# Layer norm statistics from the output tiles instead of beside the convolution taps

## The chip, the cores and the metric

The kernel runs on one core of a Trainium2 chip. What counts is the time of one execution on the device, in microseconds.

## What is computed

One layer of an encoder on two batches, 512 and 1024 tokens, with 16 meta tokens in front of each. All is in float32; matrix products are done as three products of a high and a low part.

```
u = rms_norm(h, pre_g)
z = u @ w_in                     # c_val, c_glu, c_gate, q, k, v, a_gate, 1024 columns each
y = depthwise_conv31(c_val * sigmoid(c_glu)) + conv_b
conv = silu(layer_norm(y, ln_g, ln_b)) * silu(c_gate)    # layer norm over the 1024 channels
att = neighbourhood_attention(q, k, v, rel_bias) * silu(a_gate)
out = h + rms_norm([conv ; att] @ w_out, post_g)
```

## The kernel before

In the projections and the convolution, channels lie on partitions (8 chunks `c` of 128) and the 1536 tokens lie along the free dimension, in three segments of 512. The layer norm needs a mean and a variance over channels, so over partitions and over the 8 chunks.

Stage 1, prenorm (to 100 us): the tokens are normalised, transposed and split.

Stage 2, convolution (100 to 650 us): for each chunk `c`, `stream` lets TensorE project (value, gate, the `v` of attention, the gates), while `convolve` runs the 31 taps of the chunk whose gated values `ub` are ready, each tap one pass of VectorE over 128 x 1536. The first tap (L268) and the three border copies of 15 columns (L250, L261, L262) are on ScalarE. The mean over the channels of chunk 0 is taken once by a matmul with `ones` (`conv_mean`, into `m0`); `conv_stats` subtracts it from each chunk's result (zc, which goes to DRAM as `zs`), squares that on ScalarE and adds zc and its square into `acc` and `accsq`, on GpSimd for chunks 0 to 6 and on VectorE for chunk 7. After the first projection of attention six matmuls with a column of `ones` (L538) sum both over partitions into DRAM (`std`).

Stage 3, attention (690 to 1180 us): eight pairs of heads; TensorE also projects q and k of the next pair and the gates. Results go to DRAM (`mad`). The last two gates, `a_gate(6, 7)`, are six units of 24 matmuls behind the last product with values.

Stage 4, output (from 1217 us): 12 tiles of 128 tokens. `mix` loads the sums of a tile (`moments`), the convolution half (`zs`, `cgd`) and the attention half (`mad`, `agd`) into one buffer each (`mx`, `gt`, one pair for each half), normalises, applies the gates and splits into `mh` and `ml`, which are double buffered by `t % 2`. `product` multiplies with the 16 weight blocks, whose splits (`load_wo`) are made while the last gates run. Tiles 0 and 1 are multiplied together, half by half. From tile 2 on `ml` is made on GpSimd (`MLT = 2`).

The program is traced in the order of the code; a scheduler then fixes each engine's queue by its own estimate of times. `tc.issue_after(x)` keeps the instructions of a block that are on x's engine behind x. Engines take their queues in order. All DMAs are on SP's queue.

## Time and profile before

| what | value |
|---|---|
| runs, median (lowest to highest of 3) | 1490.44 us (1488.64 to 1491.67) |
| profiled execution, its own time | 1491.02 us |
| its span, first to last instruction | 1489.2 us |
| TensorE, VectorE, ScalarE, GpSimd busy | 1444.3, 1014.3, 598.6, 321.5 us |
| mean granted TensorE clock | 0.987 of full speed |

The durations come from the profiled execution, and sums are made against its own time. A busy TensorE means that a matmul was under way; matmuls are pipelined, so the distance from start to start tells more than the duration of one.

### The profile page before, as it was taken

What the parts mean: (1) busy time and instruction counts of PE and PEld (TensorE: products, weight loads), DVE (VectorE), ACT (ScalarE), POOL (GpSimd) and SP (SyncE); (2) the same over time, 40 slices, a digit from 0 to 9 for tenths busy, and PEclk for the clock granted to TensorE, in tenths of its full rate; (3) what the DMA queues carried; (4) which work ended last, traced back from release to release, by engine and by line L of the source; (5) the groups of instructions that cost most, each with busy time, mean ns of one, the idle gap of its engine ahead of it and who ended that gap; (6) DMA issues with size and microseconds to landing.
All of it is one profiled execution on the core that took longest, in us unless ns stands there. A gap on an engine that the chain in (4) does not pass through costs nothing.

```text
span 1489.2 us, 24000 instructions
## 1 busy us (share of the span) xinstructions
PE 1444.3 (97%) x9506; PEld 1242.1 (83%) x9506; DVE 1014.3 (68%) x1713; ACT 598.6 (40%) x1323; POOL 321.5 (22%) x230
## 2 busy tenths in 40 slices
PE   7999999999989999979999999999999999999998
PEld 6988998888988887857889888888888778888886
DVE  6599989898989898974655656556555465534341
ACT  7321122111211112114545555455454576666650
POOL 2042353304220423203111110111111001221220
PEclk9999999999999999989999999999999999999999
DMA  8112213121312221213212222222122483655441
GB/s 265 38 49 92 68 49 114 40 91 47 116 46 84 68 91 57 92 50 94 64 57 73 64 63 72 75 64 73 48 78 86 154 293 114 187 144 167 121 142 43
DMA packets 124469, 138.90 MB, mean 93 GB/s; under 512 B 8110, under 2 KB 96430, under 8 KB 124356
## 3 DMA queue, kind: packets, MB, share of 16 engines
q1 hardware_dynamic: 124356, 137.36, 30.1%
q8 instruction: 74, 1.21, 0.3%
q14 instruction: 39, 0.32, 0.1%
HBM read 99.05 MB, written 42.71 MB: 95 GB/s over the span
## 4 chain that ended last, share of the span: by engine, by line
PE 61%; DVE 6%; DMA 1%; ACT 1%; POOL 1%; issue 1%; DVEq 0%; SPq 0%; ACTq 0%
PE mm L179 25%; PE py L796 18%; PE ss L615 5%; DVE z L270 4%; PE po L653 4%; PE tp L637 4%; PE tp L179 3%; PE po L179 2%; DMA wraw<-in_wo 1%; PE mm L333 1%; POOL acc L293 0%; DMA yo<-in_wo 0%; DVE accsq L294 0%; POOL accsq L294 0%; DVE uw L745 0%
## 5 line engine op out<-in xcount | busy, mean ns | idle before, releaser
L179 PE MATMUL mm<-uw,whi 128*128 128x512 f32 (+2 forms) x1904 | 559.6, 373 | 11.0 <-DVE kl L506 11.0
L270 DVE SCALAR_TENSOR_TENSOR z<-ub,cw_sb,z 128x1536 f32<-128x1536 f32 (+2 forms) x270 | 511.4, 1901 | 39.9 <-ACT z L268 31.9
L179 PEld LDWEIGHTS mm<-uw,whi 128*128 128x128 f32 x1904 | 344.2, 190 | 70.0 <-issue 13.6
L179 PE MATMUL mm<-uw,wlo 128*128 128x512 f32 (+2 forms) x952 | 354.5, 372 | 4.0 <-POOL wlo L141 4.0
L141 POOL TENSOR_TENSOR wlo<-wraw,whi 128x1024 fp32r<-128x1024 f32 x48 | 126.9, 2645 | 450.4 <-ACT whi L140 440.3
L179 PEld LDWEIGHTS mm<-uw,wlo 128*128 128x128 f32 x952 | 180.5, 190 | 32.2 <-POOL wlo L141 4.8
L796 PE MATMUL py<-uw,mh 128*128 128x512 f32 x576 | 178.4, 391 | 0.0
L179 PE MATMUL tp<-uw,whi 128*128 128x512 f32 (+2 forms) x512 | 133.9, 345 | 0.0
L626 ACT ACTIVATE pt<-pt,sm 128x216 f32<-128x216 f32 (+4 forms) x192 | 97.4, 508 | 78.4 <-DVE sm L625 76.6
L796 PEld LDWEIGHTS py<-uw,mh 128*128 128x128 f32 x576 | 108.1, 188 | 23.6
L796 PE MATMUL py<-uw,ml 128*128 128x512 f32 x288 | 112.5, 391 | 0.0
L622 DVE CUSTOM_DVE_ANT_0 pt<-ss,ei 128x216 f32<-128x216 f32 (+2 forms) x144 | 62.7, 438 | 64.8 <-PE ss L615 45.1
L639 ACT COPY pT<-tp 108x256 f32<-108x256 f32 (+4 forms) x192 | 79.3, 424 | 64.6 <-PE tp L637 55.5
L179 PEld LDWEIGHTS tp<-uw,whi 128*128 128x128 f32 x512 | 89.4, 188 | 12.1 <-issue 0.5
L776 POOL TENSOR_TENSOR ml<-mx,mh 128x1024 fp32r<-128x1024 f32 x20 | 49.2, 2480 | 218.4 <-ACT mh L775 218.4
L333 PE MATMUL mm<-vh,uw 128*128 128x256 f32 x448 | 87.6, 291 | 7.3 <-ACT vs L336 4.8
L769 DVE TENSOR_TENSOR mx<-mx,mb 128x1024 f32<-128x1024 f32 x12 | 16.8, 1399 | 104.8 <-DMA mx<-zs 104.8
L179 PE MATMUL tp<-uw,wlo 128*128 128x512 f32 (+2 forms) x256 | 88.1, 344 | 0.0
L637 PE MATMUL tp<-ident,pt 128*96 128x128 f32 (+2 forms) x480 | 87.5, 276 | 0.3
L628 DVE TENSOR_SCALAR pt<-pt,sm 128x216 f32<-128x216 f32 (+4 forms) x192 | 81.6, 427 | 5.4
L333 PEld LDWEIGHTS mm<-vh,uw 128*128 128x128 f32 x448 | 72.9, 197 | 9.3 <-ACT vs L336 5.4
L627 DVE RECIPROCAL sm<-sm 128x1 f32<-128x1 f32 x192 | 31.2, 163 | 70.1 <-ACT pt L626 67.3
(184 smaller groups left out, 2265.1 us busy)
## 6 DMA issues: line engine op xcount, KB each, us to landing
wraw<-in_w_main SPq DMA_DIRECT2D x48, 512.0 KB
xt<-in_xn SPq DMA_DIRECT2D x12, 512.0 KB
vd<-vs SPq DMA_DIRECT2D x96, 64.0 KB
cgd<-ag SPq DMA_DIRECT2D x24, 256.0 KB
zs<-zc SPq DMA_DIRECT2D x24, 256.0 KB
agd<-ag SPq DMA_DIRECT2D x24, 256.0 KB
mad<-mo SPq DMA_DIRECT2D x24, 256.0 KB
mx<-zs SPq DMA_DIRECT2D x12, 512.0 KB
```

What stands on the lines that cost most here:

```text
L141: eng.tensor_tensor(out=lo, in0=raw, in1=hi.bitcast(F32), op=ALU.subtract)
L179: last_mm[0] = nc.tensor.matmul(ps[:, :n], lhsT=w[:, dc, :], rhs=u[dc // 4][:, dc % 4, :], start=(dc == 0 and i == 0), stop=(dc == DC - 1 ...
L270: nc.vector.scalar_tensor_tensor(out=zv, in0=ub[:, a:b, k:k + 512], scalar=cw_sb[:, c, k:k + 1], in1=zv, op0=ALU.mult, op1=ALU.add)
L333: nc.tensor.matmul(ps[:, :256], lhsT=u[dc // 4][:, dc % 4, :], rhs=w[dc // 4][:, dc % 4, :], start=(dc == 0 and i == 0), stop=(dc == DC - ...
L615: last_qk[0] = nc.tensor.matmul(ss[:, :nk * w], lhsT=q[:, jj].rearrange("p h x -> p (h x)"), rhs=k[:, b0:b0 + nk, ra:ra + rn, :].rearrange ...
L622: nc.vector.tensor_tensor_reduce(out=pv.rearrange("p (k x) -> p k x", k=nk), in0=sv_, in1=e.rearrange("p k r c -> p k (r c)"), scale=1.0, ...
L626: last[0] = nc.scalar.activation(out=pv, in_=pv, func=AF.Exp, bias=sm[:, 1:2], scale=1.0, accum_out=sm[:, 2:3])
L628: nc.vector.tensor_scalar(out=pv, in0=pv, scalar1=sm[:, 3:4], scalar2=None, op0=ALU.mult)
L637: nc.tensor.transpose(out=tp[:kt, k * 128:k * 128 + 128], in_=pv[:, k * kt:k * kt + kt], identity=ident)
L639: nc.scalar.copy(out=pT[:kt, :nt * 128], in_=tp[:kt, :nt * 128])
L653: last_pv[0] = nc.tensor.matmul(po[hs, j, :], lhsT=v, rhs=pT[:kt, k * 128 + h * 64:k * 128 + h * 64 + 64], start=(k == 0), stop=(k == nt - ...
L796: nc.tensor.matmul(pss[hf], lhsT=m[e // 8][:, e % 8], rhs=w[e][:, hf * 512:hf * 512 + 512], start=(n == 0 and i == 0), stop=(n == 15 and i ...
```

## The change

The sums beside the taps go: `conv_mean`, `conv_stats`, `acc`, `accsq`, `m0`, `std` and the six matmuls. A chunk's result is only reordered by a copy on ScalarE and stored (`store_z`). In the output stage each tile's convolution half is loaded, summed over its 8 chunks by a VectorE reduction, and over partitions by a 128-column matmul with `ones` (now 1/1024), which leaves the mean on every partition; it is subtracted, the result squared on ScalarE, reduced and summed by a second matmul, and the tile is normalised (`moment_1`, `moment_2`, `normalize`). These steps for tile t+1 are put between the products of tile t, at weight blocks 2 and 10. For tiles 0 and 1 they stand between the six units of the last gates. The first tap and the border copies go to VectorE, and `ml` of the convolution half is made on VectorE in all tiles.

```diff
-                    nc.scalar.copy(out=ub[:, 1, 0:15], in_=ub[:, 0, 0:15])
+                    nc.vector.tensor_copy(out=ub[:, 1, 0:15], in_=ub[:, 0, 0:15])
...
-        nc.scalar.activation(out=zv, in_=ub[:, a:b, 0:512], func=AF.Identity, scale=cw_sb[:, c, 0:1], bias=cb_sb[:, c:c + 1])
+        nc.vector.tensor_scalar(out=zv, in0=ub[:, a:b, 0:512], scalar1=cw_sb[:, c, 0:1], scalar2=cb_sb[:, c:c + 1],
+                                op0=ALU.mult, op1=ALU.add)
...
-    def conv_mean(z):
...
-    def conv_stats(c, z, i, eng):
...
+    def store_z(c, z, i):
         zc = zpool.tile([128, 512], F32, name="zc", bufs=3)
+        nc.scalar.copy(out=zc.rearrange("p (b r c) -> p b r c", r=8, c=8), in_=z[:, i].rearrange("p (r b c) -> p b r c", r=8, b=8))
         nc.sync.dma_start(zs[i][c], zc)
...
+        if c > 0:
+            for _ in conv_taps(c, z, 0, 3):
+                yield TAP_US
+        for i in range(3):
+            store_z(c, z, i)
...
-    for i in range(3):
-        sl = slice(i * 512, i * 512 + 512)
-        for k, src in enumerate((acc, accsq)):
...
-    def moments(t):
...
-    def mix(t, parts=(0, 1)):
...
+    def channel_mean():
+
+        ps = stat[0].tile([128, 512], F32, name=stat[1], tag=stat[1])
+        nc.tensor.matmul(ps[:, :128], lhsT=ones, rhs=ms[:, 0], start=True, stop=True)
+        return ps[:, :128]
+
+    def moment_1():
+        nc.vector.tensor_reduce(out=ms[:, 0], in_=mxs[0].rearrange("p c t -> p t c"), op=ALU.add, axis=mybir.AxisListType.X)
+
+    def moment_2(t):
+        mx = mxs[0]
+        sq = wpool.tile([128, DC, 128], F32, name="wraw", tag="wraw", bufs=2)
+        mean = channel_mean()
+        nc.vector.tensor_tensor(out=mx, in0=mx, in1=mean.unsqueeze(1).broadcast_to([128, 8, 128]), op=ALU.subtract)
+        nc.scalar.activation(out=sq, in_=mx, func=AF.Square)
+        nc.vector.tensor_reduce(out=ms[:, 0], in_=sq.rearrange("p c t -> p t c"), op=ALU.add, axis=mybir.AxisListType.X)
+
+    def normalize():
+        mx, rstd = mxs[0], ms[:, 1]
+        var = channel_mean()
+        nc.scalar.activation(out=rstd, in_=var, func=AF.Sqrt, bias=eps_sb[:, 1:2])
         nc.vector.reciprocal(rstd, rstd)
...
+        (nc.gpsimd if part and t >= MLT else nc.vector).tensor_tensor(out=ml, in0=mx, in1=mh.bitcast(F32), op=ALU.subtract)
...
+    def last_gate():
+        with tc.issue_after(last_pv[0] if last_tail[0] is None else last_tail[0]):
+            next(tail, None)
+        last_tail[0] = last_mm[0]
...
+    with tc.issue_after(last[0].ins):
+        load_mix(0, 0)
+        moment_1()
+    last_gate()
+    with tc.issue_after(last_tail[0]):
+        moment_2(0)
+    last_gate()
+    with tc.issue_after(last_tail[0]):
+        normalize()
+    finish_mix(0, 0)
+    for n in range(2):
         load_wo(n)
+    last_gate()
+    load_mix(1, 0)
+    moment_1()
+    for n in range(2, 6):
+        load_wo(n)
+    last_gate()
+    with tc.issue_after(last_tail[0]):
+        moment_2(1)
+    mix_attention(0)
+    last_gate()
+    with tc.issue_after(last_tail[0]):
+        normalize()
+    last_gate()
+    finish_mix(1, 0)
...
+    def moments(t, n, first, second):
+
+        if t < TG // 128 and n in (first, second):
+            with tc.issue_after(last_y[0]):
+                if n == first:
+                    moment_2(t)
+                else:
+                    normalize()
...
+                if (part, t) == (1, 0):
+                    moments(2, n, 10, 15)
...
-            mix(t)
+            finish_mix(t, 0)
+            mix_attention(t)
+            begin_mix(t + 1)
...
             for n in range(16):
+                moments(t + 1, n, 2, 10)
                 product(t, pss, n, 0)
```

## Rows read from the trace of the kernel before

**Rows 1.** Windows by stage: TensorE, its loads, VectorE, ScalarE, GpSimd busy us (instructions); clock, DMA, GB/s.
```profile
100.00:650.00 550.00, 538.81 (x3089) 471.38 (x3088) 511.34 (x290) 101.14 (x181) 167.39 (x81) 0.99 0.23 73
650.00:690.00 40.00, 29.58 (x124) 20.91 (x125) 15.00 (x33) 14.38 (x31) 9.85 (x26) 0.83 0.28 86
...
1150.00:1217.60 67.60, 63.04 (x430) 51.75 (x429) 32.75 (x59) 37.60 (x62) 3.53 (x2) 0.95 0.63 210
1217.60:1482.60 265.00, 264.95 (x1152) 217.35 (x1152) 114.60 (x158) 153.61 (x243) 49.21 (x20) 0.99 0.46 138
```

**Rows 2.** Timeline of TensorE: start us, us, instruction, [idle before it <-what ended that].
```profile
295.45 0.38 PE L333 MATMUL mm<-vh,uw 128*128 128x256 f32 x1 [1.91 <-ACT vs L336]
...
587.20 0.80 PE L179 MATMUL mm<-uw,wlo 128*128 128x512 f32 x1 [3.50 <-POOL wlo L141]
...
660.42 0.76 PE L179 MATMUL mm<-uw,whi 128*128 128x512 f32 x1 [11.04 <-DVE kl L506]
```

**Rows 3.** Windows behind two of the four waits, columns as in rows 1 (443.6 and 587.0 repeat the first).
```profile
296.80:300.20 3.40, 3.40 (x17) 3.30 (x17) 3.33 (x3) 0.38 (x1) 0.00 (x0) 0.50 0.70 221
...
660.40:665.50 5.10, 5.08 (x12) 4.03 (x13) 0.90 (x2) 0.18 (x1) 0.00 (x0) 0.50 0.00 0
```

**Rows 4.** Timeline of VectorE and of ScalarE around the last convolution chunk.
```profile
581.15 0.68 DVE L255 TENSOR_TENSOR ub<-tp,sg 128x512 f32<-128x512 f32 x1
585.98 64.44 DVE L270 SCALAR_TENSOR_TENSOR z<-ub,cw_sb,z 128x1536 f32<-128x1536 f32 x30 [4.16 <-ACT z L268]
...
583.66 0.63 ACT L292 ACTIVATE zq<-zc 128x512 f32<-128x512 f32 x1 [3.13 <-POOL accsq L294]
...
651.24 0.63 ACT L292 ACTIVATE zq<-zc 128x512 f32<-128x512 f32 x1 [17.92 <-DVE zc L287]
```

**Rows 5.** Chain that ended last, in order of time: start us, us, what; two taps.
```profile
596.18 3.85 DVE z L270
600.05 1.83 DVE z L270
```

**Rows 6.** Timeline of TensorE: the first of the statistics matmuls and what follows the fourth.
```profile
673.99 1.02 PE L538 MATMUL ss<-acc,ones 128*1 128x512 f32 x2
...
677.51 0.50 PE L179 MATMUL mm<-uw,whi 128*128 128x512 f32 x1
```

**Rows 7.** Groups by line in one tile of the output stage: busy us, mean ns; idle before.
```profile
L796 PEld LDWEIGHTS py<-uw,mh 128*128 128x128 f32 x48 | 9.0, 188 | 1.9
...
L772 ACT ACTIVATE mx<-mx,lb_sb,lg_sb 128x128 f32<-128x128 f32 x8 | 3.2, 483 | 0.1
...
L773 ACT ACTIVATE gt<-gt 128x1024 f32<-128x1024 f32 x2 | 2.1, 1060 | 2.0 <-DMA gt<-cgd 2.0
...
L757 DVE RECIPROCAL mb<-mb 128x128 f32<-128x128 f32 x2 | 1.9, 946 | 0.5 <-ACT mb L756 0.5
...
L769 DVE TENSOR_TENSOR mx<-mx,mb 128x1024 f32<-128x1024 f32 x1 | 1.2, 1225 | 10.7 <-DMA mx<-zs 10.7
```

**Rows 8.** Timeline of SP's DMA queue and of VectorE in the output stage.
```profile
1315.48 0.36 SPq L766 DMA_DIRECT2D mx<-zs  x1
...
1319.28 1.23 DVE L769 TENSOR_TENSOR mx<-mx,mb 128x1024 f32<-128x1024 f32 x1 [12.48 <-DMA mx<-zs]
...
1233.67 0.36 SPq L766 DMA_DIRECT2D mx<-zs  x1
...
1238.83 1.23 DVE L769 TENSOR_TENSOR mx<-mx,mb 128x1024 f32<-128x1024 f32 x1 [4.33 <-DMA mx<-zs]
...
1253.62 3.31 DVE L769 TENSOR_TENSOR mx<-mx,mb 128x1024 f32<-128x1024 f32 x1 [6.38 <-DMA mx<-zs]
```

**Rows 9.** Timeline of ScalarE: a table load and the activation behind it.
```profile
1217.62 1.28 ACT L756 ACT_TABLE_LOAD   x1
1218.91 0.41 ACT L756 ACTIVATE mb<-mb,eps_sb 128x128 f32<-128x128 f32 x1
```

**Rows 10.** Groups by line, 1180 to 1218 us: a weight block's cast.
```profile
L744 ACT CAST uw<-wraw 128x1024 fp32r<-128x1024 f32 x6 | 6.3, 1052 | 5.4 <-DMA wraw<-in_wo 5.4
```

More of the change, by code (lines that the diff above doesn't have):

```diff
@@ L401, in tile_encoder @@
         pass
-    m0 = zpool.tile([128, TG], F32, name="m0")
-    acc = zpool.tile([128, TG], F32, name="acc")
-    accsq = zpool.tile([128, TG], F32, name="accsq")
-    nc.gpsimd.memset(acc, 0.0)
-    nc.gpsimd.memset(accsq, 0.0)
     def stream(c):
@@ L530, in tile_encoder @@
     pair_q(0, 0)
-    for i in range(3):
-        sl = slice(i * 512, i * 512 + 512)
-        for k, src in enumerate((acc, accsq)):
-            pool, tag = ((ps_s, "ss"), (ps_t, "tp"))[k]
-            ps = pool.tile([128, 512], F32, name=tag, tag=tag)
-            nc.tensor.matmul(ps[0:1], lhsT=ones[:, 0:1], rhs=src[:, sl], start=True, stop=True)
-            row = gpool.tile([128, 512], F32, name="ag", tag="ag", bufs=2)
-            nc.scalar.copy(out=row[0:1], in_=ps[0:1])
-            nc.sync.dma_start(std[k:k + 1, sl], row[0:1])
     es1.close()
@@ L700, in tile_encoder @@
             between(p, g * 2 + hf)
-    with tc.issue_after(last_pv[0]):
-        for _ in a_gate(6, 7):
-            pass
     es2.close()
-    es_ps.close()
-    ps_y = ctx.enter_context(tc.tile_pool(name="ps_y", bufs=6, space=bass.MemoryType.PSUM, reuse_waits="tile"))
     wop = ctx.enter_context(tc.tile_pool(name="wop", bufs=1, reuse_waits="tile"))
@@ L778, in tile_encoder, with load_mix @@
[L778 to L788 removed]
+    stat = [ps_s, "ss"]
+    def load_mix(t, part):
+        g, csl = t // 4, slice(t % 4 * 128, t % 4 * 128 + 128)
+        nc.sync.dma_start(mxs[part], (zs, mad)[part][g][:, :, csl].rearrange("c p t -> p c t"))
+        nc.sync.dma_start(gts[part], (cgd, agd)[part][g][:, :, csl].rearrange("c p t -> p c t"))
@@ new lines, in normalize, with finish_mix @@
+    def normalize():
+        mx, rstd = mxs[0], ms[:, 1]
+        var = channel_mean()
+        nc.scalar.activation(out=rstd, in_=var, func=AF.Sqrt, bias=eps_sb[:, 1:2])
+        nc.vector.reciprocal(rstd, rstd)
+        nc.vector.tensor_tensor(out=mx, in0=mx, in1=ms[:, 1:2].broadcast_to([128, 8, 128]), op=ALU.mult)
+        for c in range(8):
+            nc.scalar.activation(out=mx[:, c], in_=mx[:, c], func=AF.Silu, scale=lg_sb[:, c:c + 1], bias=lb_sb[:, c:c + 1])
+    def finish_mix(t, part):
+        mx, gt = mxs[part], gts[part]
+        mh, ml = [x[t % 2 * 2 + part] for x in (mhs, mls)]
+        nc.scalar.activation(out=gt, in_=gt, func=AF.Silu)
+        nc.vector.tensor_tensor(out=mx, in0=mx, in1=gt, op=ALU.mult)
+        nc.scalar.copy(out=mh, in_=mx)
+        (nc.gpsimd if part and t >= MLT else nc.vector).tensor_tensor(out=ml, in0=mx, in1=mh.bitcast(F32), op=ALU.subtract)
@@ new lines, in tile_encoder @@
+    finish_mix(0, 0)
+    for n in range(2):
+        load_wo(n)
+    last_gate()
[12 more added lines that the diff above has]
+    finish_mix(1, 0)
+    for n in range(6, 10):
+        load_wo(n)
+    mix_attention(1)
+    for n in range(10, 16):
+        load_wo(n)
```

89 lines of the change are left out of this document (20 added, 69 removed).

## Prediction

> **What bounds the kernel now.** I read the windows by stage first, then the rows around each place where TensorE stands, and last one tile of the output stage. The windows show that TensorE is nearly always busy, and where it is not: the convolution stage (100 to 650 us) leaves it 11.2 us idle, the 40 us behind it 10.4 us, the passage into the output stage 4.6 us, and the output stage nothing, 264.95 of 265.0 us [rows 1]. So time can be won only where TensorE waits, runs at half clock, or does work that goes away, and every microsecond put in front of it later is lost again.
>
> The waits stand at the ends of convolution chunks. At 587.20 a weight load waits 3.50 us for GpSimd's weight split, at 295.45 a value projection waits 1.91 us for a PSUM copy on ScalarE (the same, 1.90 us, stands at 443.25), and at 660.42 the K projection waits 11.04 us for VectorE [rows 2]. Behind each such wait the granted clock reads 0.50, the lower level of 1.2 GHz, for 3.4 us, and for 5.1 us behind the last [rows 3]. Why they wait is seen in the chunk's end: GpSimd adds zc and its square into accumulators, ScalarE's second Square waits 3.13 us for that, and the first tap stands behind the Square on ScalarE; VectorE waits 4.16 us for it. The 30 taps then take 64.44 us, and behind them come the subtraction and, on VectorE, the last accumulations; ScalarE stood 17.92 us behind the Square that needs them, with the K evictions queued after it [rows 4].
>
> **The change, part by part.** It removes first taps (8) and Squares (24) from ScalarE, 24 subtractions and 6 accumulations from VectorE, 42 accumulations from GpSimd, and 18 matmul records from TensorE. It adds 8 first taps and 24 border copies to VectorE, 24 reordering copies to ScalarE, and in the output stage, for each of 12 tiles, two reductions, a subtraction and a Square, and two matmuls of 128 columns with `ones`.
>
> *End of chunks, gain.* With GpSimd's accumulators gone, nothing on ScalarE stands between the last gated piece and the first tap. The three earlier waits make 1.91 + 1.90 + 3.50 = 7.3 us, and half of 3 x 3.4 us at half clock is 5.1 us: 12.4 us. For chunk 7: VectorE's last gated piece ends at 581.8 [rows 4], and 30 taps at the undisturbed pitch of 1.86 us would be 55.7 us; the 8.7 us beyond that come with the weight splits on GpSimd (a tap of 3.85 us instead of 1.83 while one ran [rows 5]), of which four remain, some 8 us. The first tap on VectorE has no row; the two-input tap of 1536 elements took 1.83 us, which bounds it from above; with the border copies I take 1.5. So the taps end near 581.8 + 1.5 + 55.7 + 8 = 647, instead of 650.4, and 9 us of subtraction and accumulation no longer follow. TensorE, 5 us earlier itself, comes to this point at about 644 instead of 649. What is late next is ScalarE: the three copies that store z wait for the last tap in its queue, with the K evictions behind them, about 2 us. I therefore leave 3 us of the 11.04 and drop the half clock behind it (half of 5.1): 10.6 us. Bounds for this block: 10 us (only the early waits go) to 26 us (everything goes). Taken: 23.0 us.
>
> *Matmuls removed.* Four records with `accsq` and `acc` follow each other from 673.99 to 677.51, 0.44 us a record, 12 of them [rows 6]; the six of the mean have the same 512 columns: 18 x 0.44 = 7.9 us, all on TensorE's queue while it is otherwise full.
>
> *Work added under cover.* Border copies and first taps (8 x 1.5 = 12 us) go to VectorE, which stands idle for 39 of 550 us of the convolution stage [rows 1] and loses the subtractions. The cover is the taps finishing before TensorE needs the K evictions; without it each us there is a us.
>
> *Matmuls added.* 24 times two records of 128 columns. By columns, a quarter of 2 x 0.44 is 0.22 us; with both weight loads of 0.19 us [rows 7] in the open, 0.60. TensorE loads ahead, but a load is longer than the 0.11 us of such a record, so I take 0.40: 9.6 us (5.3 to 14.4).
>
> *Tile loop of the output stage.* This decides the sign. The statistics of tile t+1 are inserted in TensorE's queue while it multiplies tile t, and all of it goes through one buffer mx. The chain from one first statistics matmul to the next: to the second one 8 steps of three products at 265.0 / 1152 = 0.23 us plus one statistics matmul, 5.9 us (the subtraction 1.23, a Square like the Silu of 1.06, and a reduction priced like a two-input pass, 1.22, fit in that). Then the matmul's result 0.45 (an estimate from its 0.40), Sqrt 0.41 [rows 9], reciprocal 0.95, product 1.22, eight Silus 3.2, gate product 1.22 [rows 7], cast 1.05 [rows 10], ml 1.22: 9.7 us; then the load of the next mx, and a reduction, 1.2 again; with the handovers 17.1 us and the load. The load took 3.80 us from issue (1315.48) to use, and 5.16 from 1233.67 beside another load [rows 8]. Sum: 20.9 to 22.3 us. TensorE's tile takes 22.1 + 0.8 = 22.9. So the loop fits, but with 0.6 to 2.0 us to spare, and the queues hold other work: the attention half, the output's squares, gains and sums, and the ml of the attention half on GpSimd, beside which a 1.23 us pass of VectorE took 3.31 [rows 8]. I take 0.6 us of stall on each of 9 tiles, 5 us (0 to 30).
>
> A table load stands in that loop twice, Sqrt and then Silu. ScalarE's row shows 1.28 us each [rows 9], and the second fits under the reciprocal and product (2.2 us), so I charge nothing. By the Trainium skill ("ScalarE: Activation LUTs", What ACT_TABLE_LOAD costs) a switch is about 2.66 us with its drain; as an estimate from that page the loop would be 0.5 us longer and the forecast 4 us later, inside its own range. The trace does not agree: behind the load at 1217.62 the next activation starts at 1218.91 [rows 9].
>
> *Passage into the output stage.* Before, tile 0's convolution half is mixed during attention; now its Square, second reduction and normalisation come between the six gate units of 5.5 us, and tile 1's behind them. These passes share VectorE and ScalarE with the splitting of 16 weight blocks (a cast of 1.05 us and a subtraction of 1.22 each) and the transfers with their loads (six casts wait 5.4 us for them) [rows 10]. Tile 0: second statistics matmul after the second unit (11 us), normalised and split 10 to 12 us later, at 23; load of mx under those loads 6, reduction 1.3, at 30; two statistics matmuls and their chain 15 more, at 46 to 49. Tile 1's first product is due behind 34.5 us (six units and four statistics matmuls) and tile 0's 11, at 45.5. I take 4 us (0 to 10). SP's queue loses 12 loads and 6 stores of sums and gains none.
>
> *Sum.* On the profiled execution's 1491.0 us: -23.0 - 7.9 + 9.6 + 5 + 4 = -12.3, 1478.7; the runs' median is 0.6 below that execution: 1478 us.
>
> **Rivals.** (1) *The mx loop sets the tile period* (slower). Place: first statistics matmul of tile t+1, with products queued behind it. Every us of load and queueing beyond 5.8 costs 9. The gain ahead of it is 30.9 - 9.6 - 4 = 17.3 us, so it decides from 1.9 us more, 7.7 in all. For it: VectorE already waits 10.7 us in a tile for mx in this stage [rows 7]. Against it: that wait holds up nothing on TensorE today, and two loads in a row gave 5.2. At 8.5 to 9: 1478 - 5 + 27 = 1500 us. The Trainium skill ("TensorE: Matmul & The Clock Gate", Part 2) says that matmuls stay in program order and only weight loads are pulled ahead; by it the waiting statistics matmul holds all products behind it, as the row at 587.20 shows for a late weight.
>
> (2) *The end of the convolution keeps its wait.* If the store copies hold ScalarE until the last tap as the Square does now, and the taps stay near 64 us, only the early waits and the matmuls go: 10.6 us less gain, 1489. For it: 17.92 us of that wait is waiting for taps. Against: the chunk starts 4 us earlier and 9 us behind the taps go.
>
> (3) *Everything fits.* No stall in the loop, none in the passage, statistics matmuls at 0.25 us, all 26 us of waits: 1491 - 26 - 7.9 + 6 = 1463 less 0.6, 1462 us. For it: the loop's bare sum is below the period. Against: it needs every queue to be free at the right moment.
>
> **How the numbers follow.** Forecast, 1468 to 1486: 0.45. Rival 1, 1486 to 1515: 0.22. Rival 2, 1484 to 1493: 0.16. Rival 3, below 1468: 0.17. About 0.2% (3 us) is what a measurement of this kernel can tell from no change, so faster ends at 1487.5 and slower begins at 1493.4. Faster: all of the forecast and rival 3, 0.04 of rival 2, 0.03 of rival 1, 0.69. Same: the other 0.12 of rival 2. Slower: the other 0.19 of rival 1. The range is 1460 to 1500: it takes in more than half of rival 3, rival 2 and the lower half of rival 1, and leaves out 0.18; the forecast's own is 1468 to 1486.
>
> **What would show it.** Right: no wait over 3 us on TensorE between 100 and 690, no granted 0.50 there, taps of chunk 7 ending by 647; the attention stage some 460 us as before; in the output stage gaps below 1 us before the first statistics matmul of a tile, and a tile period near 23 us. Wrong: a tile period of 24 us or more with VectorE's reduction waiting for mx (rival 1); ScalarE waiting over 10 us in front of a store copy while K evictions are due (rival 2); or a wait over 6 us between gate units, where tile 1's statistics stand.

## The result, and the profile after

The changed kernel takes 1539.63 us (median of 4 runs, 1539.29 to 1540.18), the kernel before 1489.95 beside it: a ratio of 1.0332, 95% interval 1.0319 to 1.0345. The forecast was 1478 us, range 1460 to 1500.

Three instants of TensorE split the time: the last product with values of attention, the first product of the output stage, and the last one (the first and last start of these lines' records in each trace). Between the first two lie the last six gates, the passage.

| kernel | last product with values | passage | output products |
|---|---|---|---|
| before | 1180.6 | 37.0 | 264.6 |
| forecast, by its terms | 30.9 earlier | 5.6 longer | 13 longer |
| after | 1142.4, 38.2 earlier | 46.1, 9.1 longer | 342.8, 78.2 longer |

So the first half of the forecast came out, 7 us better than said, and the second missed by 69 us, 65 of them in the loop over tiles. Windows by stage of the kernel after, columns as in rows 1:

```profile
100.00:650.00 550.00, 548.84 (x3174) 481.91 (x3174) 500.41 (x317) 97.95 (x174) 111.81 (x69) 1.00 0.26 81
650.00:690.00 40.00, 40.00 (x280) 34.35 (x278) 24.34 (x102) 21.14 (x62) 7.79 (x8) 1.00 0.19 55
...
1150.00:1217.60 67.60, 56.22 (x241) 45.67 (x241) 43.50 (x35) 42.69 (x56) 0.00 (x0) 0.92 0.68 219
1217.60:1537.60 320.00, 267.06 (x1073) 211.09 (x1071) 153.63 (x149) 151.91 (x237) 24.39 (x10) 0.91 0.31 96
```

In the convolution TensorE has lost its 21.6 us of idle time [rows 1] but for 1.2, and the clock stands at 1.00. In the output stage it is busy 267.06 of 320 us, and the mean granted clock is 0.91, where it was 0.99 [rows 1].

One tile of the output stage, from one load of mx to the next; timelines of the kernel after, SP's DMA queue, VectorE, then TensorE:

```profile
1419.04 0.36 SPq L705 DMA_DIRECT2D mx<-zs  x1
...
1449.07 0.36 SPq L705 DMA_DIRECT2D mx<-zs  x1
...
1425.77 1.99 DVE L715 TENSOR_REDUCE ms<-mx 128x128 f32<-128x1024 f32 x1 [3.35 <-DMA mx<-zs]
1429.38 1.22 DVE L721 TENSOR_TENSOR mx<-mx,st 128x1024 f32<-128x1024 f32 x1 [1.63 <-PE st L711]
1431.95 2.01 DVE L723 TENSOR_REDUCE ms<-wraw 128x128 f32<-128x1024 f32 x1 [1.35 <-ACT wraw L722]
...
1443.83 1.23 DVE L738 TENSOR_TENSOR mx<-mx,gt 128x1024 f32<-128x1024 f32 x1 [3.26 <-ACT mx L732]
1445.35 1.97 DVE L858 TENSOR_TENSOR s<-s 128x1 f32<-128x1 f32 x1 [0.29 <-ACT ag L801]
1447.24 0.68 DVE L805 TENSOR_TENSOR yo<-py,pgb 128x512 f32<-128x512 f32 x1
1447.84 1.21 DVE L740 TENSOR_TENSOR ml<-mx,mh 128x1024 fp32r<-128x1024 f32 x1
...
1428.96 0.38 PE L711 MATMUL st<-ms,ones 128*128 128x128 f32 x2
1437.54 0.38 PE L711 MATMUL st<-ms,ones 128*128 128x128 f32 x2
1446.30 0.50 PE L796 MATMUL py<-woh,mh 128*128 128x512 f32 x1 [3.13 <-ACT mh L739]
1449.10 0.80 PE L796 MATMUL py<-woh,ml 128*128 128x512 f32 x1 [1.60 <-DVE ml L740]
```

The loop closes: 30.0 us from load to load, and nothing in it overlaps with its own next turn, since the next load starts when `ml` ends (1449.05 and 1449.07). Five pieces make up the turn, each set against its term in the prediction; the last column but one is the mean of nine turns (30.5 us), read from the same timelines:

| piece | rows | measured | mean of nine | forecast |
|---|---|---|---|---|
| load, issue to use | 1419.04 to 1425.77 | 6.7 | 5.8 | 3.8 to 5.2 |
| first reduction | 1.99 | 2.0 | 2.0 | 1.2 |
| to the first statistics matmul | 1427.76 to 1428.96 | 1.2 | 2.0 | 0.3 for all handovers |
| first to second matmul | 1428.96 to 1437.54 | 8.6 | 8.6 | 5.9 |
| second matmul to the end of ml | to 1449.05 | 11.5 | 12.0 | 9.7 |

The second reduction ended at 1433.96, but 36 products stand between the two matmuls in TensorE's queue, where the code asks for at least 24: 3.6 us are lost waiting for a place. The first matmul, too, stands 37 products into the tile where the code asks for at least 6. At the end the split `ml`, whose result opens both TensorE's next products and the next load, stands behind the previous tile's sum of squares `s` (one column, 1.97 us) and a gain (0.68): it starts 2.8 us after the gated product and 1.6 us after the cast mh, on which it waits as well, has ended (1445.22 + 1.03, timeline of ScalarE). And the load is issued 1.75 us behind the attention half's load (1417.29, timeline of SP's queue), beside which the prediction had seen 5.2 us at most. Two of the nine turns are longer, 33.0 and 34.3 us: there ScalarE's queue has the cast of the attention half, which waits 2.5 us for TensorE, ahead of the Silus.

The passage is 9.1 us longer by two waits of TensorE at tile 1's statistics matmuls; timeline of TensorE after:

```profile
1180.51 0.49 PE L711 MATMUL ss<-ms,ones 128*128 128x128 f32 x2 [4.29 <-DVE ms L715]
1188.09 0.80 PE L711 MATMUL ss<-ms,ones 128*128 128x128 f32 x2 [7.09 <-DVE ms L723]
```

### The profile page after: what moved, and what is told of

It is laid out like the page before. It is cut to its first block, busy times and chain, and to the rows that moved or that the text cites. A ratio compares the mean times of both kernels' runs of the same rounds, so it can differ in the third digit from the quotient of the medians.

```text
span 1537.6 us, 23911 instructions
## 1 busy us (share of the span) xinstructions
PE 1458.0 (95%) x9536; PEld 1250.4 (81%) x9536; DVE 1047.9 (68%) x1714; ACT 596.8 (39%) x1297; POOL 228.0 (15%) x176
## 4 chain that ended last, share of the span: by engine, by line
PE 82%; DVE 5%; issue 5%; ACT 4%; DMA 3%; POOL 1%; DVEq 0%; SPq 0%; ACTq 0%; POOLq 0%
PE mm L177 34%; PE py L796 15%; PE tp L177 8%; PE ss L574 5%; PE po L177 5%; PE po L612 4%; PE tp L596 3%; PE mm L318 3%; PE tp L318 3%; ACT mx L732 1%; DVE s L858 1%; POOL vl L139 1%; DVE ml L740 1%; ACT mh L739 1%; PE po L318 1%
## 5 line engine op out<-in xcount | busy, mean ns | idle before, releaser
L269 DVE SCALAR_TENSOR_TENSOR z<-ub,cw_sb,z 128x1536 f32<-128x1536 f32 (+2 forms) x270 | 497.4, 1849 | 8.1
L139 POOL TENSOR_TENSOR wlo<-wraw,whi 128x1024 fp32r<-128x1024 f32 x48 | 132.4, 2760 | 603.1 <-ACT whi L138 598.4
L796 PE MATMUL py<-uw,mh 128*128 128x512 f32 x576 | 189.2, 409 | 0.0
L796 PEld LDWEIGHTS py<-uw,mh 128*128 128x128 f32 x576 | 114.7, 200 | 25.9
L796 PE MATMUL py<-uw,ml 128*128 128x512 f32 x288 | 117.1, 407 | 0.0
L318 PE MATMUL mm<-vh,uw 128*128 128x256 f32 x448 | 84.5, 285 | 0.8 <-ACT uw L202 0.8
L177 PE MATMUL po<-uw,whi 128*128 128x512 f32 (+2 forms) x272 | 73.1, 348 | 0.0
L138 ACT CAST whi<-wraw 128x1024 fp32r<-128x1024 f32 x48 | 50.4, 1051 | 55.3 <-DMA wraw<-in_w_main 18.0
```

The source lines that it names most:

```text
L139: eng.tensor_tensor(out=lo, in0=raw, in1=hi.bitcast(F32), op=ALU.subtract)
L177: last_mm[0] = nc.tensor.matmul(ps[:, :n], lhsT=w[:, dc, :], rhs=u[dc // 4][:, dc % 4, :], start=(dc == 0 and i == 0), stop=(dc == DC - 1 ...
L269: nc.vector.scalar_tensor_tensor(out=zv, in0=ub[:, a:b, k:k + 512], scalar=cw_sb[:, c, k:k + 1], in1=zv, op0=ALU.mult, op1=ALU.add)
L318: nc.tensor.matmul(ps[:, :256], lhsT=u[dc // 4][:, dc % 4, :], rhs=w[dc // 4][:, dc % 4, :], start=(dc == 0 and i == 0), stop=(dc == DC - ...
L796: last_y[0] = nc.tensor.matmul(pss[hf], lhsT=m[e // 8][:, e % 8], rhs=w[e][:, hf * 512:hf * 512 + 512], start=(n == 0 and i == 0), stop=(n ...
```

## The experiments

The first theory was rival 1 at a larger price: one buffer, held from load to split, makes the chain of a tile serial with the next one's. The rivals to it: the places of instructions in the engines' queues, and the work itself. Each kernel ran beside the kernel before, whose median lay between 1488.7 and 1490.7 us and whose single runs lay between 1487.2 and 1492.7. A kernel that was run once is therefore known to some 3 us.

**What the statistics cost in all.** The changed kernel without them (`moment_1` and `moment_2` empty, `normalize` only the eight Silus).

> The changed kernel without the statistics: the two reductions, the subtraction of the mean, the squares, the statistics matmuls, square root, reciprocal and the product with them are left out (so the mix goes to the Silu unnormalized); load, Silu, gate and splits stay, with one buffer. It says what a statistics stage that costs nothing would give. Theory (the chain through the statistics is what makes the 86.7 us): load 5.95, Silu 3.2, gate 1.4, cast 1.4 and split 2.6 are 14.6 us in a period of 23 to 24, so the whole of 72 us in the tiles and 13 in the passage comes back: 1450 to 1460 us. Rival: part of the loss is the transfers' or the split's beside GpSimd and stays: 1470 to 1500 us.

Measured: 1450.73 us (one run); passage 33.1, products 263.0. So the chain of load, Silu, gate and split fits with its one buffer, and statistics in the output stage cost 89 us of the 1539.6, in the passage (33.1 against 46.1) as in the products (263.0 against 342.8); attention ended 4 us later there. The convolution's gain stands by itself.

**One part alone: taps and border copies on VectorE, the rest as before.**

```diff
-        nc.scalar.activation(out=zv, in_=ub[:, a:b, 0:512], func=AF.Identity, scale=cw_sb[:, c, 0:1], bias=cb_sb[:, c:c + 1])
+        nc.vector.tensor_scalar(out=zv, in0=ub[:, a:b, 0:512], scalar1=cw_sb[:, c, 0:1], scalar2=cb_sb[:, c:c + 1],
+                                op0=ALU.mult, op1=ALU.add)
...
```

> The kernel before, with the first tap and the border copies on VectorE and nothing else: the statistics stay beside the taps. Its output stage is that of before, so whatever the changed kernel lost from the passage on (395.0 us after the last gates start, 308.3 before) can't appear. The theory says that the 38.3 us by which the last gates start earlier in the changed kernel come in part from the first tap (ScalarE frees 3.85 us per chunk, TensorE waited 4.16 us for it at the last chunk) and for the larger part from the statistics that stood at the end of the last chunk (17.92 and 3.13 us): 1470 to 1482 us, so 8 to 20 us faster than before. Rival: the whole gain comes from the statistics leaving the taps, then this stays at 1487 to 1492. Second rival: the taps alone carry it, 1450 to 1455.

Measured: 1489.06 us, ratio 0.9993 (0.9984 to 1.0003): nothing, the rival's case. (The 4.16 us were VectorE's wait, not TensorE's [rows 4].) **The other part alone**, the changed kernel with that line and the border copies back on ScalarE:

> The changed kernel with the first tap and the border copies back on ScalarE, that is the move of the statistics alone. The taps alone gave nothing (1489.1 us; VectorE was busy for 541.6 of the 550 us from 100 to 650, 511.3 before). Theory: the 38 us that the conv stage gained come from the statistics that left VectorE, GpSimd and ScalarE there, and the first tap matters little by itself: 1537 to 1546 us. Rival: the two only work together (with the first tap on ScalarE TensorE still waits for it at the chunk's end): 1550 to 1565 us. Second rival: the first tap on VectorE costs more than it gives, also here: 1525 to 1535 us.

Measured: 1542.0 us (one run); the last product with values starts at 1142.4, as in the changed kernel. Windows of the convolution and the stretch behind it, taps alone first, then statistics alone, each from its own trace:

```profile
100.00:650.00 550.00, 535.56 (x3075) 467.48 (x3074) 541.60 (x322) 88.52 (x156) 175.95 (x81) 0.99 0.24 74
650.00:690.00 40.00, 32.54 (x149) 23.86 (x150) 14.28 (x40) 14.50 (x35) 10.64 (x28) 0.87 0.34 89
```

```profile
100.00:650.00 550.00, 549.46 (x3179) 482.59 (x3178) 484.29 (x291) 112.56 (x202) 109.64 (x69) 1.00 0.26 81
650.00:690.00 40.00, 40.00 (x293) 34.22 (x294) 24.34 (x101) 21.41 (x63) 7.81 (x8) 1.00 0.19 55
```

The 38 us are the statistics' alone. With taps and statistics both on it, VectorE is busy for 541.60 of 550 us, and TensorE stands idle for 21.9 us in the two stretches, as before (21.6).

**The places of the statistics matmuls.** The changed kernel; the products of a tile are kept behind the matmuls, which then stand at 6 and 30 products.

```diff
...
-                product(t, pss, n, 0)
+                with tc.issue_after(last_stat[0]):
+                    product(t, pss, n, 0)
...
-                product(t, pss, n, 1)
+                with tc.issue_after(half_end):
+                    product(t, pss, n, 1)
```

> The changed kernel, with the products of a tile tied behind the two statistics matmuls of the next one, so that these stand 6 and 30 products into each tile (33 to 50 and 36 more before). Theory of the loop (one buffer is held from the load to the last split, and load, two reductions, two matmuls and the chain behind them follow each other): the second matmul was ready 3.5 us before it ran, so the period falls from 30.1 to about 26.6 us, and TensorE now waits at the first matmul instead of at the products; 9 tiles by 3.5 us: 1500 to 1515 us. Rival, the order alone: with the matmuls early the period is TensorE's own 24 to 24.5 us: 1480 to 1492 us. Rival, the work itself (VectorE's instructions stretched beside GpSimd and the transfers): nothing moves, 1535 to 1542 us.

Measured: 1490.58 us (one run), products 294.6: of the 78.2 us, 48.2 came back without a buffer, an engine or an instruction changed. That is the rival's number, not the first theory's. Timelines of VectorE and TensorE of this kernel:

```profile
1320.36 1.20 DVE L722 TENSOR_TENSOR mx<-mx,st 128x1024 f32<-128x1024 f32 x1
...
1323.00 1.88 DVE L724 TENSOR_REDUCE ms<-wraw 128x128 f32<-128x1024 f32 x1
...
1317.60 0.38 PE L712 MATMUL st<-ms,ones 128*128 128x128 f32 x2
1324.94 0.49 PE L712 MATMUL st<-ms,ones 128*128 128x128 f32 x2 [1.47 <-DVE ms L724]
```

The tile is down to 24.2 us, 1.3 above TensorE's own 22.9, with waits of some 1.4 us at the second matmul. But more than TensorE's order has changed, for the scheduler laid out the other queues anew with it. Means of the last seven turns, in us, from the timelines of both kernels:

| piece | changed kernel | matmuls at 6 and 30 |
|---|---|---|
| load, issue to use | 5.9 | 4.1 |
| first reduction | 2.0 | 2.0 |
| to the first statistics matmul | 2.0 | 0.5 |
| first to second matmul | 8.6 | 7.3 |
| second matmul to the end of ml | 12.0 | 10.1 |
| turn | 30.5 | 24.1 |

The waits of the two matmuls for their places give 2.8 of the 6.4 us. The rest is the load, which is no longer issued behind the attention half's, and the end of the turn, where VectorE now takes `s` ahead of the subtraction (1317.92) and not ahead of `ml`. So the run shows what the order of the queues is worth together; it does not separate the queues.

**The buffer.** Two tries: the gated product written into the gate's buffer, so that mx is free before cast and split; and a second buffer for the mix.

```diff
-        nc.vector.tensor_tensor(out=mx, in0=mx, in1=gt, op=ALU.mult)
+        nc.vector.tensor_tensor(out=gt, in0=mx, in1=gt, op=ALU.mult)
```

> The changed kernel, with the gated product written into the gate's own buffer: the buffer of the mix is free when the gate product has been taken (1445.2 us in the tile of 1419 us) and not after the split (1449.1 us). The same instructions run. Theory of the loop: the load of the next tile starts 3.9 us earlier in each of 9 tiles, 1500 to 1510 us. Rival, the order: as long as the statistics matmuls stand where they do nothing is gained, over 1530 us. Rival, the work itself: 1535 to 1542 us.

```diff
+            mixes[t] = mxs[0] if t < 2 else wpool.tile([128, DC, 128], F32, name="wraw", tag="wraw", bufs=2)
...
+        sq = mxs[0] if t > 1 else wpool.tile([128, DC, 128], F32, name="wraw", tag="wraw", bufs=2)
```

> The changed kernel with two buffers for the mix from the third tile on (they take the two slots of the staging tile, and the squares go where the mix was); the same instructions on the same engines. Theory of the loop: load, reduction and subtraction of a tile no longer wait for the split of the tile before, so the chain has about two periods; the period falls from 30.1 us to TensorE's own 24 to 24.6, and with it the half clock leaves: of the 72 us that the nine tiles lost nearly all comes back, the passage's 13 us stay: 1465 to 1480 us, faster than before. Rival, the work itself: VectorE and ScalarE are what sets the period, then the second buffer brings little: over 1520 us. Rival, the order: the matmuls stand 8 and 46 products into the tile, and the chain after the second (11.5 us) still ends after the tile's last products: 1495 to 1515 us.

Measured: 1513.10 us (one run) and 1492.28 us, ratio to before 1.0018 (1.0008 to 1.0028). The first is 3 us above the theory's case: the load starts earlier, but the first matmul then waits 5.1 to 5.6 us for its place in six of the last seven turns, and the turn shrinks by 2 us, not by 3.9. The second is far from it: with the load out of the loop, TensorE still waits 14.3 us in 8 waits for the cast mh, because the chain behind the second matmul, 46 to 48 products into the tile, ends after the tile's last product. It came out below the 1495 to 1515 of the rival on order, but by that rival's mechanism.

**Both, and then one trip instead of two.** The two remedies together, the matmuls at 9 and 39 products; and beyond that mean and mean square taken at once (Square, two reductions, one matmul of 256 columns; the variance is their difference).

> The changed kernel with both remedies: two buffers for the mix from the third tile on, and the products tied behind the statistics matmuls, now 9 and 39 products into each tile. The order alone gave 1490.6 us, the second buffer alone 1492.3. Theory (two limits in parallel: the chain behind the second matmul has to fit ahead of the tile's end, and the load and the first reduction ahead of the first matmul; each remedy lifts one): reduction 1 is ready when a tile begins, the second matmul stands 9 us into the tile and 11.5 us of chain follow, 20.5 of 23 us; of the tiles' loss 3 to 8 us stay, the passage's 13 stay: 1463 to 1473 us. Rival: VectorE, busy for 21 to 27 of each 40 us and serving in order, delays the chain anyhow, and the two remedies don't add: 1482 to 1492 us.

> The kernel with both remedies, with the mean and the mean square taken from the load at once: square, two reductions and one matmul of 256 columns per tile, then the variance as mean square less the square of the mean. One wait of TensorE for the statistics per tile in place of two. Theory: the tiles' loss is gone as in the kernel with both remedies, and the passage, where TensorE waited 7.1 and 4.3 us at the two matmuls of the second tile, loses one of its two waits: 3 to 8 us under the kernel with both remedies, 1456 to 1468 us. Rival: the two reductions now follow each other (4 us) ahead of the one matmul, and the passage waits as long at one place: the same time as that kernel within 2 us.

Measured: 1487.18 us, 0.9977 (0.9966 to 0.9987), and 1483.68 us, 0.9957 (0.9943 to 0.9971). The remedies don't add: 49 and 47 us each, 52 together. For the first kernel the rival on VectorE's order holds, for the second neither case does; timelines of VectorE and TensorE in the kernel with both:

```profile
1314.57 1.92 DVE L865 TENSOR_TENSOR s<-s 128x1 f32<-128x1 f32 x1 [4.57 <-ACT ag L805]
1316.42 0.68 DVE L809 TENSOR_TENSOR yo<-py,pgb 128x512 f32<-128x512 f32 x1
...
1317.09 1.20 DVE L725 TENSOR_TENSOR wraw<-wraw,st 128x1024 f32<-128x1024 f32 x1
...
1311.78 0.38 PE L715 MATMUL st<-ms,ones 128*128 128x128 f32 x2
1321.44 0.49 PE L715 MATMUL st<-ms,ones 128*128 128x128 f32 x2 [2.43 <-DVE ms L727]
```

The mean was there at 1312.2, and VectorE idle, but the head of its queue was `s`, which waits for the end of the tile before; the subtraction starts 4.9 us later, and TensorE waits at the second matmul. One trip took 7.5 us out of the passage (38.6 us) and gave 5.5 back in the loop (292.8 against 287.3), where, among other waits, weight blocks are now late for the first products (4.4 us).

**Reductions and the split.** The reductions as three additions, and (in another kernel) `MLT = 12`, which moves the attention half's split from GpSimd to VectorE.

> The changed kernel with each reduction over the eight channels (2.0 us) written as three additions of 512, 256 and 128 elements (0.69 us for 512 elements, so about 1.3 together). Theory: the first reduction stands in the chain from the load to the first matmul and gives its 0.7 us per tile, the second ends ahead of the second matmul's place anyhow: 9 tiles by 0.7: 1530 to 1536 us. Rival: the length of the two reductions is what made the tile long, 9 by 1.4 and the half clock with it: 1515 to 1528 us. Second rival: no change, 1537 to 1542 us.

> The changed kernel with the split of the attention half on VectorE (1.25 us) instead of GpSimd (2.49 us) in all tiles. Theory: beside GpSimd's split a VectorE instruction of one column took 1.97 us instead of 0.15 and held up the split of the mix, which opens the next load; that goes and 1.25 us come on VectorE: 0.5 to 1 us per tile, 1530 to 1536 us. Rival: the meeting of VectorE and GpSimd is a main part of the tile's excess: 1505 to 1525 us. Second rival: VectorE is the limit and its 1.25 us more per tile show: 1545 to 1555 us.

Measured: 1547.09 and 1516.11 us (one run each). The additions took 0.69 + 0.42 + 0.29 = 1.4 us instead of 2.0, and the kernel got 7.5 us slower: the scheduler laid the queues out anew, 38 to 41 products now stand between the two matmuls instead of 36, and TensorE's waits for mh grew from 37.9 to 47.6 us. So shorter reductions bring nothing if the places get worse; as the layout changed with them, the run doesn't isolate their length. The split gave 23.5 us, far more than 9 times the theory's 1, and in the range of the rival, the meeting of VectorE and GpSimd. VectorE's timeline there, from the gated product of the mix to its `ml`:

```profile
1342.90 1.22 DVE L738 TENSOR_TENSOR mx<-mx,gt 128x1024 f32<-128x1024 f32 x1 [3.26 <-ACT mx L732]
1344.05 1.22 DVE L740 TENSOR_TENSOR ml<-mx,mh 128x1024 fp32r<-128x1024 f32 x1
1345.18 0.15 DVE L858 TENSOR_TENSOR s<-s 128x1 f32<-128x1 f32 x1
1345.25 0.68 DVE L805 TENSOR_TENSOR yo<-py,pgb 128x512 f32<-128x512 f32 x1
1345.85 1.22 DVE L740 TENSOR_TENSOR ml<-mx,mh 128x1024 fp32r<-128x1024 f32 x1
```

The `ml` at 1344.05 is the attention half's, now on VectorE; the mix's is the one at 1345.85, behind which the next load is issued (1347.10). It still stands behind `s` and the gain, but `s` takes 0.15 us, and `ml` starts 1.7 us after the gated product instead of 2.8. In the changed kernel `s` took 1.86 to 1.99 us in the eight of twelve tiles in which GpSimd's split had begun some 0.5 us before it, and ended when the split did (1447.32 and 1447.30 in the tile above); in the other four it took 0.15. So here the order on VectorE stayed, and the length of `s` beside GpSimd went. A turn takes 27.7 us instead of 30.5 (means of the last seven), 1.4 of it less at the end and 1.2 less in front of the first matmul. At the end, turns like the one above became 1.0 us shorter (11.5 to 10.5), and the two long turns of the changed kernel, in which ScalarE's queue is in another order, are gone. How the 23.5 us divide between the meeting and the new layout isn't shown. Two kernels asked whether that adds to the other remedies:

> The changed kernel with one buffer, the products tied behind the statistics matmuls (6 and 30 products into a tile, alone 1490.6 us) and the split of the attention half on VectorE (alone 1516.1 us). If the late place of the matmuls and the meeting of VectorE and GpSimd are two losses that add: 1490.6 less most of 23.5, bounded by what the passage and the matmuls still cost: 1468 to 1474 us. If both lengthen the one chain, of which only what stands over TensorE's own 23 us shows: 1480 to 1488 us, with TensorE waiting 0.5 to 1.5 us per tile at the second matmul.

> The kernel with two buffers, fixed order and one trip of the statistics (1483.7 us), with the split of the attention half on VectorE in all tiles. Theory: what the tiles still lose there (some 1.5 to 2.5 us each, TensorE waiting for the cast and the split) comes from VectorE's instructions that stretch beside GpSimd (1.91 us for one of one column): 8 tiles by 1 to 1.5: 1471 to 1477 us. Rival: VectorE, now with 1.25 us more per tile and serving in order, is late by as much as it wins: 1482 to 1488 us.

Measured: 1502.89 us (one run), slower than with the order alone, which neither case foresaw; and 1481.43 us, 0.9939 (0.9921 to 0.9956), less of a gain than the theory asked and half a microsecond outside the rival's range. In the first, VectorE's queue holds a gate product of the attention half between subtraction and second reduction:

```profile
1322.05 1.20 DVE L722 TENSOR_TENSOR mx<-mx,st 128x1024 f32<-128x1024 f32 x1
...
1325.67 1.23 DVE L739 TENSOR_TENSOR mx<-mx,gt 128x1024 f32<-128x1024 f32 x1 [0.90 <-DMA mx<-mad]
1326.81 1.86 DVE L724 TENSOR_REDUCE ms<-wraw 128x128 f32<-128x1024 f32 x1
```

It waits for a load, the reduction waits behind it, and TensorE waits 2.4 us at the matmul where the kernel with the order alone waited 1.4.

**The gain without the loss.** The kernel before, its statistics still beside the taps but off VectorE, except for the squares of the last chunk: chunks copied by ScalarE as they are, no mean of chunk 0.

```diff
...
-                          in1=m0[:, sl].rearrange("p (b r c) -> p b r c", r=8, c=8), op=ALU.subtract)
+        nc.scalar.copy(out=zc.rearrange("p (b r c) -> p b r c", r=8, c=8), in_=z[:, i].rearrange("p (r b c) -> p b r c", r=8, b=8))
...
-        eng.tensor_tensor(out=acc[:, sl], in0=acc[:, sl], in1=zc, op=ALU.add)
+        nc.gpsimd.tensor_tensor(out=acc[:, sl], in0=acc[:, sl], in1=zc, op=ALU.add)
```

> The kernel before (statistics beside the taps, output stage and first tap as they were), in which the statistics cost VectorE next to nothing: the chunk is copied out by ScalarE as it is (no mean of the first chunk is taken and subtracted), squared on ScalarE and added on GpSimd; only the squares of the last chunk are added on VectorE. Theory: the conv stage is bound by VectorE (511.3 of 550 us busy before, 541.6 with the first tap and no gain; 484.3 and TensorE at 549.5 with the statistics gone), so what counts is that the subtractions and the last chunk's additions leave VectorE: most of the 38 us come, less the six matmuls that stay, and the output stage costs nothing extra: 1455 to 1468 us. Rival: GpSimd's additions slow the taps beside them (1.90 us each before against 1.85 in the changed kernel, some 210 of them), and VectorE stays the bound: 1470 to 1482 us. Second rival: the last chunk's sums are late for the six matmuls, and TensorE waits there: 1480 to 1492 us.

Measured: 1478.86 us, ratio 0.9931 (0.9917 to 0.9944): faster than both kernels, but 10 us faster than before where 21 to 34 were expected, in the first rival's range. Two of TensorE's waits (us in total, times, longest), and under them the group of VectorE's taps (busy us, mean ns; idle before them):

```profile
PE mm L179 <- POOL wlo L141: 7.4, 2, 6.8
PE mm L179 <- DVE kl L492: 5.6, 1, 5.6
```

```profile
L270 DVE SCALAR_TENSOR_TENSOR z<-ub,cw_sb,z 128x1536 f32<-128x1536 f32 (+2 forms) x270 | 511.5, 1901 | 49.9 <-ACT z L268 41.8
```

These three stalls (a weight split behind additions on GpSimd, a key split behind additions on VectorE, VectorE's 41.8 us of waiting for first taps, 31.9 in the kernel before) were then taken away together:

> The kernel before with the statistics copied out, squared and added off VectorE (1478.9 us), and its three remaining stalls taken away: the first tap and the border copies on VectorE (VectorE waited 4.3 us for the first tap of the last chunk, behind ScalarE's squares), the additions of a chunk behind the weight split that GpSimd has to do first and eight taps apart (TensorE waited 6.8 us for that split), the last chunk's additions on GpSimd behind the first key projections (TensorE waited 5.6 us for a split of the keys behind VectorE's additions). Theory: what the conv stage gained by the change is VectorE's and GpSimd's time at the chunk's end and nothing else, so it can be had without touching the output stage: of the 22 us that this conv stage still loses against the changed kernel's 10 to 18 come: 1461 to 1469 us. Rival: VectorE is bound again (484 us of taps and products, 15 of first taps, and taps stretched beside 48 additions): 1473 to 1485 us.

Measured: 1481.26 us, 0.9940 (0.9922 to 0.9959), no better: the rival. Groups of the taps and of GpSimd's additions in this kernel, then the taps in the changed kernel:

```profile
L273 DVE SCALAR_TENSOR_TENSOR z<-ub,cw_sb,z 128x1536 f32<-128x1536 f32 (+2 forms) x270 | 538.1, 2000 | 8.1
L292 POOL TENSOR_TENSOR accsq<-accsq,zq 128x512 f32<-128x512 f32 x24 | 59.2, 2467 | 0.6 <-ACT zq L286 0.6
L291 POOL TENSOR_TENSOR acc<-acc,zc 128x512 f32<-128x512 f32 x24 | 57.5, 2397 | 55.2 <-ACT zc L283 55.2
```

```profile
L269 DVE SCALAR_TENSOR_TENSOR z<-ub,cw_sb,z 128x1536 f32<-128x1536 f32 (+2 forms) x270 | 497.4, 1849 | 8.1
```

The wait for first taps is gone, and the same 270 taps take 41 us more beside GpSimd's 48 additions. Laid beside each other, the timelines show the additions under the taps for some 104 us in this kernel and for some 24 us in the one before it, where most of them stood in VectorE's pauses: what was taken from the waits came back in the taps. Last, the sums were moved to the attention stage, from what the convolution had stored, with the output stage of before; and once more with the transposes' buffer restored and the sums' matmuls a step later.

```diff
+        nc.sync.dma_start(zl, zs[t // 4][2 * c:2 * c + 2, :, t % 4 * 128:t % 4 * 128 + 128].rearrange("c p t -> p c t"))
...
+                nc.scalar.activation(out=zl, in_=zl, func=AF.Square)
...
+                    nc.gpsimd.tensor_tensor(out=src, in0=src, in1=zl[:, i], op=ALU.add)
```

> The conv stage of the changed kernel (chunks copied out unsummed, first tap on VectorE), the output stage of the kernel before (mean and variance read as sums from memory), and the sums taken in between, beside the attention blocks, from what the conv stage stored: per token tile four loads of two channel blocks, squares on ScalarE, additions on GpSimd (66 of the 410 us from 690 to 1100 busy before), two matmuls of 128 columns and two rows stored. One buffer of the attention's transposes is given up for the sums. Theory: the change's 38 us came from the conv stage and its loss of 86.7 us only from statistics in the output stage; with the sums where engines have room both halves are had: 1489 less 38, plus 24 matmuls at about 0.3 and what the loads and GpSimd disturb: 1453 to 1466 us. Rival: TensorE stands at 408.9 of 410 us in that stretch and the attention's chain through VectorE and ScalarE has no slack; GpSimd's 168 additions and the lost buffer stall it: 1470 to 1490 us.

> The kernel with the sums beside the attention (1557.4 us), with its two named stalls lifted: the transposes have their fourth buffer back (TensorE waited 14.6 us for it; a bias buffer is given up instead), and the two matmuls of a token tile are placed one attention step (some 10 us) after its last additions (TensorE waited 24.3 and 2.2 us for these). Theory (those two stalls, with the half clock that follows them, are the whole excess over the forecast): the attention stretch comes back to within 10 us of its old length: 1460 to 1475 us. Rival: the stage has no room for the work at all: squares, loads through the score buffers and GpSimd's additions stand in the softmax chain, and most of the 95 us stays: over 1520 us.

Measured: 1557.43 us, 1.0444 (1.0423 to 1.0465), and 1499.93 us, 1.0074 (1.0055 to 1.0093). TensorE's waits, the first kernel above, the second below:

```profile
PE ss L657 <- POOL acc L654: 24.3, 9, 5.2
PE tp L598 <- ACT pT L600: 14.6, 15, 2.6
```

```profile
PE tp L598 <- ACT pT L600: 12.8, 16, 2.8
...
PE ss L660 <- POOL acc L655: 2.4, 3, 1.2
```

The first lies above both cases of its expectation. From 690 to 1182 us TensorE stands idle for 47.3 us in the first kernel and for 24.4 in the second, at mean granted clocks of 0.95 and 0.99; in the kernel before it is 3.6 us at 1.00 (windows of the three traces). The waits for sums fell from 26.5 us (24.3, and 2.2 for accsq) to 2.4, those for transposes only from 14.6 to 12.8. That speaks for the early matmuls as the larger part of the loss and against the buffer, though the two were changed in one kernel. Neither case of the last expectation holds: 57 us came back, and some 40 stay, since the last product with values starts at 1182.0 instead of the changed kernel's 1142.4; behind it the passage is 40.2 us, 3 longer than before. TensorE being full in that stage, the sums found no free place there in this form either.

## Why the prediction was wrong

*End of chunks* (forecast 23.0, with the removed matmuls 30.9; measured 38.2): the sign and most of the size were right, the account only in part. It gave the gain to ScalarE's queue and costed the first tap on VectorE as part of the remedy. The two one-part kernels show that the tap's move gives nothing by itself and isn't needed. It put the last taps' end near 647, counting chunk 7 alone; they ended at 617.5 (from 559.50 on, 28 taps in 58.03 us): every chunk before had become shorter too, chunk 7 starts 30 us earlier than at 585.98 [rows 4], and TensorE doesn't wait there. It left 3 us of the 11.04 standing, and they went as well: TensorE's idle time fell by 20.4 us (21.6 to 1.2) where the terms counted 15.3. With 7.9 us for the matmuls, as forecast, the block gave 30.3, above its own bound of 26. Its sign, no wait over 3 us from 100 to 690, came true (one of 1.2 us, clock 1.00), and rival 2 fell.

*Matmuls added* (0.40 us for a pair of records): the pair's records span 0.38 us in the tile above. Not the error.

*Tile loop* (5 us; measured 78.2 less 8 for the matmuls, 70): the step that failed. The sentence "the loop fits, but with 0.6 to 2.0 us to spare" came from terms that were each short: 20.9 to 22.3 us against 30.0 in the tile above. The reductions were priced as a two-input pass, 1.2 instead of 2.0. The others were priced as if nothing stood ahead of them in a queue. The second matmul was given 24 products behind the first and got 36; the first was to run at once and waited 2.0 us on the mean; the load was issued right behind another and took 5.8; and `ml` was priced at its own 1.22 us behind the cast, without the previous tile's `s` and gain ahead of it, and without the stretch of `s` beside GpSimd. Laying the queues out in another order brought 49 us with the same instructions, and taking GpSimd's split away 23.5 us, each in one run; shorter reductions in a worse layout brought nothing. All of this lengthens one chain, so the remedies don't add. Rival 1 had the right place, and its sign (a period over 24 us, the reduction waiting for mx) showed; its break-even (1.9 us more per tile) was passed by far, at 7.1 us over TensorE's 22.9, but its price of 1500 us held only what an 8.5 to 9 us handover costs. The prediction also listed the other work in the queues, GpSimd's split among it, and then charged 0.6 us per tile for all of it. That is the judgement that was wrong; its own upper bound of 30 us was too low as well.

*Passage* (4 us, 0 to 10, and 1.6 for matmuls; measured 9.1): right place, tile 1's matmuls, and two waits of 11.4 us together, where TensorE stood idle for 4.6 us before [rows 1]. One of them is 7.09 us, so the sign that the prediction had named for this (a wait over 6 us between gate units) showed. The kernel with one trip took 7.5 us out of the passage, which bears the place out.

The rule of program order on TensorE, cited with rival 1 from the Trainium skill ("TensorE: Matmul & The Clock Gate", Part 2), agrees with the trace: the statistics matmul whose input was there at 1433.96 runs at 1437.54, behind the products ahead of it. The prediction used the rule only for products behind a waiting matmul; it holds a ready matmul behind products as well, and that was missed.

What stays open: how the 49 us divide among the queues of TensorE, VectorE and SP, and the 23.5 us between the meeting with GpSimd and the layout; why shorter reductions led to a layout 7.5 us slower, beyond that the queues came out differently; and which of the small waits beside attention could be removed.

## What to carry to other kernels

Before a latency chain is threaded through a full engine's queue, write down for each link what stands ahead of it in the queue of every engine that it passes, as the compiled order has it, not as the code's minimum allows. When several links wait for places, removing one moves the wait to the next: try the free remedy (the order) first and measure, since buffers and faster passes may then buy nothing. And test a change's parts alone: here one part was worth 38 us, one nothing, and one cost 89.

## What the runs showed of the hardware

- A reduction of 128x1024 to 128x128 over a strided view took 1.98 us (mean of 12), where a two-input pass over the same elements took 1.22; written as three additions it took 1.4.
- A VectorE addition of one column took 1.86 to 1.99 us in the eight tiles of the changed kernel in which GpSimd's 2.4 to 2.5 us split had begun some 0.5 us before it, and 0.15 in the other four and in the kernel that has no such split (mean of 12).
- GpSimd's additions of 128x512 took 1.3 to 1.7 us where no tap ran on VectorE, and 2.0 to 2.8 beside the taps, mostly 2.8 in the kernel with 48. The same taps took 1.85 us each with no such additions, 1.90 with 42 that stood mostly in the pauses between the taps (kernel before), and 2.00 with 48 that were spread over them.
- The load of a 128x1024 tile took 5.6 to 6.7 us from issue to use where the attention half's load was issued 1.75 us ahead of it (five turns of the changed kernel), and 3.6 to 4.6 us where no load of the attention half was issued within 9 us ahead of it (last seven turns of the kernel with the matmuls at 6 and 30).
